# A hybrid DeltaNet and attention layer on one core: gates and rotation from PSUM, a mask by TensorE, wider spacing of dependent products, and a last stage one tile ahead

## The chip, the core and the metric

The kernel runs on one core of a Trainium2 chip. TensorE multiplies into PSUM, VectorE and ScalarE read PSUM, GpSimd works on SBUF only, and SyncE's queue starts most DMA transfers. The metric is device time per execution, in microseconds (us): 1606.91, the median of three runs (1602.01, 1608.14, 1606.91). Lower is better.

## The reference, cut to what matters

```python
mod = silu(c) @ w_mod + b_mod                    # shift, scale, gate
h = rmsnorm(x, norm_w) * (1 + scale) + shift     # (2048, 1024)
proj = h @ w_in      # DeltaNet q,k,v and gate z, its beta and decay, attention q,k,v and gate z
dn_qkv = silu(causal_short_conv(dn_qkv, conv_w)) # 4 heads x 128; q and k are l2-normalised
o_dn = gated_delta_rule(q, k, v, g, beta)        # per chunk: decay exp(g_c - g_s) for s <= c,
                                                 # inverse of a unit triangular matrix, state S
o_dn = rmsnorm(o_dn, dn_norm_w) * silu(dn_z)
aq, ak = rope(at_q, positions), rope(at_k, positions)
o_at = dilated_attention(aq, ak, av)             # 8 heads x 64, windows with strides 1, 4, 16, joined by log-sum-exp
o_at = rmsnorm(o_at, at_norm_w) * silu(at_z)
x = x + gate * (concat(o_dn, o_at) @ w_out)
return rmsnorm(x, final_norm_w)
```

Everything is float32. The kernel takes a large product as three: each operand is split into a part `hi` that float32r holds exactly and a rest `lo`, and hi*hi, hi*lo and lo*hi are added up in PSUM.

## The kernel before

The 2048 tokens are taken in two halves of two blocks of 512. There are four stages.

- **Start** (to about 160 us): modulation, normalised x, first projections.
- **Projections with DeltaNet** (to about 1095 us): the main stream, `rest` and `dn_unit`, makes one projection after another, each 24 products of 128x128 by 128x512 into a bank `ip` (two buffers). Sixteen DeltaNet units (4 heads x 4 blocks) run beside it.
- **Hand-over** (to about 1135 us): `mix_first` multiplies `NM` token tiles of the DeltaNet output by w_out, 24 products a tile, and adds x; attention's operands are loaded.
- **Attention** (to about 1495 us) and the **last stage**: `attention` runs 128 pieces of scores, softmax, transposes and values. `mix_dn` (the DeltaNet tiles that `mix_first` left) and then `mix_at` (the attention half of the output, final RMSNorm, 16 tiles) are generators in the queue `side`, stepped beside it as `FILL` says, and alone once attention is out of pieces.

A DeltaNet unit is a chain of small dependent products: `dn_intra` (decay matrix, gram products), `dn_solve` (16x16 inverses on VectorE), `dn_double` (inverse doubled to 32, 64 and 128 in TensorE products named `g<-...`), and `dn_scan` (four chunks, each `sc<-state,kq`, then `sc<-y,inv`, then `sc<-y,kdec` and `sc<-y,qk`; VectorE or ScalarE makes the next operand in between), then `dn_out`. Each part sits in a queue of its own; `tick` steps the first generator of each queue once per step of the main stream. Between dependent products a generator waits in `hop(n)` until the main stream has issued n x 1.1 us of estimated TensorE work (`spent`), or, where the main stream has nothing to issue, 0.3 us of such credit per tick. A unit may not start its projections before the unit four places earlier is through (`done[0] < n - KQ + 1`), and waits in `dn_intra` until its set of buffers is free (`u["need"]`). A scheduler then orders the instructions by its own model of when each can start, so the final order differs from the order of the code. Each engine works through its own in order.

Names that the change touches: `DB0`, `DB1`, `DB2`, `SC1`, `SC2`, `SC3` are the n of the hops of `dn_double` and `dn_scan`; `z_gate` makes silu(z) from a projection's bank; `rope_unit` rotates q and k; `gate_row` computes the modulation's gate.

Of the kernel before, what the change touches and what calls it, by code (L numbers as in the profile page):

```python
# [11 lines left out]
F32 = mybir.dt.float32  # L12
# [9 lines left out]
P = 128  # L22
# [17 lines left out]
DB0 = 2.5  # L40
DB1 = 2.0
DB2 = 2.0
SC1 = 2.5
SC2 = 1.5
SC3 = 1.5
# [11 lines left out]
NM = 4  # L57
# [32 lines left out]
FILL = (1, 0)  # L90
# [22 lines left out]
def kernel(ctx: ExitStack, tc: tile.TileContext, x, c_t, pos, w_mod, b_mod_t, b_gate,  # L113
# [110 lines left out]
    gt_r = persist.tile([P, P], F32R, name="gt_r")  # L224
    cw = persist.tile([P, 12, 4], F32, name="cw")
# [457 lines left out]
    def z_gate(pool, ps, col, dst):  # L683

        zr = pool.tile([P, J], F32, name="z_r", tag="t512", bufs=T5)
# [116 lines left out]

    def dn_double(pool, u, xct):
# [17 lines left out]
        yield from hop(DB1)  # L821
# [10 lines left out]
        yield from hop(DB0)  # L832
        for lvl in range(2):
# [14 lines left out]
            yield from hop(DB1)  # L848
# [8 lines left out]
            yield from hop(DB2)  # L857
        grown[0] += 1

    def dn_scan(fa, pool, h, j, u, gt_, gz):  # L860
# [6 lines left out]
        for c in range(4):  # L867
# [6 lines left out]
            yield from hop(SC1)  # L874
# [3 lines left out]
            yield from hop(SC2)  # L878
# [7 lines left out]
            yield from hop(SC3)  # L886
        tail.append(dn_out(fa, pool, h, j, o, so, u["eq"], gz))

    def dn_out(fa, pool, h, j, o, so, eq, gz):
# [13 lines left out]
        V.tensor_tensor(oc, ps.rearrange("p c t -> p (c t)").rearrange("p (i r) -> p r i", r=4),  # L903
                        g.rearrange("p (r i) -> p r i", r=4), OP.mult)
# [28 lines left out]
    def dn_unit(fa, h, js, hs, gt_, launch, ahead=None):  # L933
        wk, wv = [load_unit(2 * h + i) for i in range(2)] if not ahead else (None, ahead[0])
        for jj in range(2):
# [16 lines left out]
            z_gate(fa, (yield from proj(wv, hs[jj], 1)), 0, gz)  # L952
# [30 lines left out]
    def z_part(pool, u, j, ct, ps):  # L983
        gz = pool.tile([P, J], F32, name="z_at", tag="t512", bufs=T5)
        z_gate(pool, ps, 1, gz)
# [12 lines left out]
    def rope_unit(fa, u, js, hs, w):  # L998
        w = w or load_unit(u)
        scr = (qscr, kscr)[u >= 10][u % 2]  # L1000
        for jj in range(2):
# [6 lines left out]
            xs = []  # L1008
            for ct in range(2):
                ps = yield from proj(w, hs[jj], ct)  # L1010
                t = fa.tile([P, J], F32, name="rx", tag="t512", bufs=T5)
                A.copy(t.rearrange("p (r i) -> p r i", r=4), ps.rearrange("p (i r) -> p r i", r=4))  # L1012
                xs.append(t)
                yield
            for ct in range(2):
                p1 = fa.tile([P, J], F32, name="rp1", tag="t512", bufs=T5)
                p2 = fa.tile([P, J], F32, name="rp2", tag="t512", bufs=T5)
                V.tensor_tensor(p1, xs[ct], tab[0], OP.mult)
# [222 lines left out]
    def combine(pool, p, blk, oa, ob, sta, sb):  # L1241
# [47 lines left out]
        V.tensor_tensor(oc, ps, flat(gz), OP.mult)  # L1289
# [150 lines left out]
    for half in range(2):  # L1440
# [6 lines left out]
        for h in range(HD):  # L1447
            run(dn_unit(fa, h, js, hs, gts[half], launch, None if half or h else (wv, kqs)))
            if half == 0 and h == 1:
# [64 lines left out]
    with tc.tile_pool(name="mix", bufs=2, side="right", reuse_waits="tile") as mp:  # L1514
        with tc.tile_pool(name="att", bufs=2, side="left", reuse_waits="tile") as ap_:
# [32 lines left out]
            def mix_at():  # L1548
# [8 lines left out]
                yield from hop(MIXLAG2)  # L1557
                for i in range(16):
                    t = 4 * (i % 4) + i // 4
                    while combined[i // 4] < 4:  # L1560
                        yield
                    y = ya[:, i % 4]
                    dma(y, yscr[t // 4, (t % 4) * P:(t % 4 + 1) * P, :])
                    ss = ap_.tile([P, 4], F32, name="f_ss", bufs=4)

                    def use(n, ps):
# [3 lines left out]
                        A.activation(sq, y[:, c], AF.Square, accum_out=ss[:, n:n + 1])  # L1570
                        if n == 0:
                            V.tensor_scalar(ss[:, 0:1], ss[:, 0:1], 1.0 / D, EPS, op0=OP.mult, op1=OP.add)

                    oc = yb[:, 1 + i // 2 % 3, i % 2 * J:i % 2 * J + J].rearrange("p (k i) -> p k i", k=4)
                    yield from mix(*halves("m_x", MX), load_o(oc, t, 4), wa, use, lambda: bank("s", SB) if over else bank("ip", IP2))
                    V.scalar_tensor_tensor(ss[:, 2:3], ss[:, 1:2], 1.0 / D, ss[:, 0:1], op0=OP.mult, op1=OP.add)
                    G.tensor_tensor(y[:, J:D], y[:, J:D], fw[:, J:D], OP.mult)
                    rsqrt(ap_, ss[:, 3:4], ss[:, 2:3], "f")
                    V.scalar_tensor_tensor(y[:, 0:J], y[:, 0:J], ss[:, 3:4], fw[:, 0:J], op0=OP.mult, op1=OP.mult)  # L1579
                    A.activation(y[:, J:D], y[:, J:D], AF.Copy, scale=ss[:, 3:4])  # L1580
                    for c in ((slice(0, J), slice(J, D)) if i == 15 else (slice(0, D),)):
                        nc.scalar.dma_start(class_rows(t, out)[:, c], y[:, c])
# [104 lines left out]
```

## Time and profile before

| | |
|---|---|
| profiled execution, its own time | 1607.58 us (span of its instructions 1605.7) |
| median of three runs | 1606.91 us |
| TensorE products (PE) | 1448.7 us busy, 90% of the span |
| VectorE (DVE) | 1125.1 us, 70% |
| ScalarE (ACT) | 674.5 us, 42% |
| GpSimd (POOL) | 497.7 us, 31% |
| mean granted TensorE clock | 0.963 of full |

Busy PE counts each product from start to end, and neighbours overlap; the time from one product to the next is shorter than its duration. A wait of PE in the rows is idle time, put down to what ended it. [...]

### The profile page before, as it was taken

To read this page: it belongs to the slowest core of one execution; us is meant where nothing else is said; L and a number is where in the kernel's file an instruction comes from. 1 tells how busy PE (TensorE), PEld (TensorE's weight loads), DVE (VectorE), ACT (ScalarE), POOL (GpSimd) and SP (SyncE) were. 2 spreads that over 40 slices of the span, in tenths; PEclk is the share of its full clock that TensorE was granted. 3 is DMA by queue.
4 is the path that set the end of the run, shared out by engine and by line. 5 is a ranking of instruction groups with operands and counts; after the bars stand their busy time and mean duration, and the time that the engine had idled before them with its cause. 6 is when DMAs were issued, how large, how long until landed. Compare 5 with 4: busy or idle time off the path is not lost. (4 is left out here: it accounts for less than half of the span.)

```text
span 1605.7 us, 28520 instructions
## 1 busy us (share of the span) xinstructions
PE 1448.7 (90%) x9832; PEld 1166.6 (73%) x9832; DVE 1125.1 (70%) x3478; ACT 674.5 (42%) x1894; POOL 497.7 (31%) x589
## 2 busy tenths in 40 slices
PE   3898899799879878999999999997899999999986
PEld 3686778667667767877877688876677777777764
DVE  6858825796775776676777767435476686898887
ACT  3534224324233664424324243222455555666443
POOL 2324352354462424133142321213121221142333
PEclk9989999999999988999999999998999999999998
DMA  8745551755552652161442424437877637264353
GB/s 253 255 134 177 163 170 56 246 165 179 166 183 89 222 160 90 53 191 57 147 139 79 149 74 148 148 114 237 252 214 214 198 109 235 82 197 113 120 191 129
DMA packets 255184, 252.89 MB, mean 157 GB/s; under 512 B 44864, under 2 KB 196544, under 8 KB 254528
## 3 DMA queue, kind: packets, MB, share of 16 engines
q1 hardware_dynamic: 252592, 242.69, 48.8%
q10 hardware_dynamic: 2448, 8.39, 1.3%
q8 instruction: 78, 1.28, 0.3%
q14 instruction: 66, 0.54, 0.1%
HBM read 160.12 MB, written 90.90 MB: 156 GB/s over the span
## 5 line engine op out<-in xcount | busy, mean ns | idle before, releaser
L149 PE MATMUL ip<-h_hi,w_hi 128*128 128x512 f32 x864 | 355.9, 413 | 1.5 <-ACT z_r L689 1.5
L149 PE MATMUL ip<-h_hi,w_lo 128*128 128x512 f32 x864 | 355.8, 413 | 0.0
L149 PE MATMUL ip<-h_lo,w_hi 128*128 128x512 f32 x864 | 354.5, 412 | 0.0
L149 PEld LDWEIGHTS ip<-h_hi,w_hi 128*128 128x128 f32 x864 | 167.1, 194 | 33.8 <-ACT z_r L689 2.2
L149 PEld LDWEIGHTS ip<-h_hi,w_lo 128*128 128x128 f32 x864 | 166.6, 193 | 32.3 <-issue 0.5
L149 PEld LDWEIGHTS ip<-h_lo,w_hi 128*128 128x128 f32 x864 | 166.9, 193 | 31.9 <-issue 0.2
L675 DVE SCALAR_TENSOR_TENSOR cv_y<-cv_r,cw,cv_y 128x512 f32<-128x512 f32 x144 | 117.1, 813 | 41.0 <-ACT cv_y L672 37.1
L561 POOL TENSOR_TENSOR w_lo<-w_raw,w_hi 128x512 fp32r<-128x512 f32 x72 | 98.1, 1372 | 128.3 <-ACT w_hi L560 106.3
L1204 DVE CUSTOM_DVE_ANT_0 sm<-s,mask 128x256 f32<-128x256 f32 (+3 forms) x256 | 107.8, 446 | 19.3 <-PE s L149 14.0
L154 PE MATMUL tr<-cst,p 128*128 128x128 f32 x568 | 94.3, 287 | 3.4 <-ACT p L1207 1.7
L1229 DVE COPY pts<-tr 128x512 f32<-128x512 f32 (+1 forms) x120 | 72.9, 615 | 33.7 <-PE tr L154 32.6
L1207 ACT ACTIVATE p<-sm,sta 128x256 f32<-128x256 f32 (+1 forms) x128 | 63.2, 495 | 71.2 <-DVE sta L1204 60.4
L1207 ACT ACTIVATE p<-sm,stb 128x128 f32<-128x128 f32 (+3 forms) x128 | 70.9, 555 | 50.2 <-DVE stb L1204 37.3
L154 PEld LDWEIGHTS tr<-cst,p 128*128 128x128 f32 x568 | 61.7, 142 | 25.0 <-issue 15.8
L149 PE MATMUL ip<-w_hi,h_hi 128*128 128x264 f32 (+1 forms) x256 | 76.8, 300 | 2.8 <-ACT v_at L138 1.5
L149 PE MATMUL ip<-w_hi,h_lo 128*128 128x264 f32 (+1 forms) x256 | 76.9, 300 | 0.0
L149 PE MATMUL ip<-w_lo,h_hi 128*128 128x264 f32 (+1 forms) x256 | 76.8, 300 | 0.0
L789 DVE TENSOR_TENSOR tmp_inv<-xt_inv,blk 128x8 f32<-128x8 f32 (+14 forms) x240 | 67.2, 280 | 5.8
L677 ACT ACTIVATE cv_t<-cv_y 128x512 f32<-128x512 f32 x48 | 30.3, 632 | 82.9 <-DVE cv_y L675 62.3
L560 ACT CAST w_hi<-w_raw 128x512 fp32r<-128x512 f32 x72 | 43.5, 619 | 50.6 <-DMA w_raw<-in_w_in_dram 25.8
L1019 POOL TENSOR_TENSOR rp<-rx,tab 128x512 f32<-128x512 f32 x32 | 43.3, 1366 | 58.0 <-ACT rx L1012 51.2
L138 ACT ACTIVATE sqo<-o 128x128 f32<-128x128 f32 x64 | 19.8, 309 | 93.4 <-DVE o L138 84.0
(464 smaller groups left out, 3497.3 us busy)
## 6 DMA issues: line engine op xcount, KB each, us to landing
w_raw<-in_w_in_dram SPq DMA_DIRECT2D x72, 256.0 KB, 4.0
ws<-w_hi SPq DMA_DIRECT2D x15, 1024.0 KB, 5.5
ws<-w_lo SPq DMA_DIRECT2D x15, 1024.0 KB, 7.1
w_hi<-ws SPq DMA_DIRECT2D x15, 1024.0 KB, 5.8
w_lo<-ws SPq DMA_DIRECT2D x15, 1024.0 KB, 7.4
xt<-in_x_dram SPq DMA_DIRECT2D x16, 512.0 KB, 4.7
wm<-in_w_mod_dram SPq DMA_DIRECT2D x32, 256.0 KB, 5.5
tab<-ctab SPq DMA_DIRECT2D x32, 256.0 KB, 3.5
```

The lines of the kernel that those rows point to most:

```text
L138: return f(*a, **k)
L149: i = self.engine.matmul(ps, lhsT=lhsT, rhs=rhs, **k)
L154: i = self.engine.transpose(*a)
L560: A.copy(hi[:, s, 0:256], raw)
L561: G.tensor_tensor(lo[:, s, 0:256], raw, hi[:, s, 0:256], OP.subtract)
L675: V.scalar_tensor_tensor(y, r[:, n:n + J], cw[:, ti, n:n + 1], y, op0=OP.mult, op1=OP.add)
L677: A.activation(t, y, AF.Tanh)
L789: V.tensor_tensor(tmp[:, :, 0:i + 1], xt[:, :, 0:i + 1], b3[:, i:i + 1, 0:i + 1].to_broadcast([P, 4, i + 1]), OP.mult)
L1019: G.tensor_tensor(p2, xs[1 - ct], tab[1], OP.mult)
L1204: V.tensor_tensor_reduce(out=sm, in0=pp[hd], in1=masks, scale=-0.125, scalar=BIG, op0=OP.add, op1=OP.min, accum_out=st[:, slot, hd:hd + 1])
L1207: A.activation(pt, sm, AF.Exp, scale=-1.0, bias=st[:, slot, hd:hd + 1], accum_out=st[:, slot, 2 + hd:3 + hd])
L1229: V.tensor_copy(pts[:, 0:kn], pt[:, 0:kn])
```

## The change

1. `z_gate`: ScalarE's copy of the bank (scaled by a norm weight) goes; VectorE's product reads the bank itself. The norm weight is applied in `dn_out` and `combine`, where a two-operand product becomes a three-operand one.
2. `rope_unit`: the product with the cosines is made from the bank right after the projection; ScalarE's copy stays for the other product.
3. `dn_intra`: GpSimd's multiplication of the decay matrix by a triangular mask goes; a third product into the same bank, of -1e30 times the identity with the strict triangle, sends the masked exponents to minus infinity before the exponential.
4. The hops of `dn_double` and `dn_scan` grow for the units 0 to 13: doubling from 2.0 (one 2.5) to 4.0, scan from 2.5, 1.5 and 1.5 to 4.0, 3.0 and 3.5. The last two units keep the short ones.
5. `mix_first` takes eight tiles and not four (`NM`), and beside attention every third step works on `side`, not every second (`FILL`).
6. `mix_at` loads and splits tile i+1 before the products of tile i, and makes the final norm's reciprocal roots for two tiles at once.
7. `gate_row` moves from the second head of the first half to the first head of the second half.

```diff
-DB0 = 2.5
-DB1 = 2.0
-DB2 = 2.0
-SC1 = 2.5
-SC2 = 1.5
-SC3 = 1.5
+DB = (4.0, 2.0)
+SC1 = (4.0, 2.5)
+SC2 = (3.0, 1.5)
+SC3 = (3.5, 1.5)
+SHORT = 14
-NM = 4
+NM = 8
-FILL = (1, 0)
+FILL = (1, 0, 0)
...
+        V.tensor_scalar(off_r, ident, -1.0e30, None, op0=OP.mult)
...
     def z_gate
         A.activation(t.rearrange("p (r i) -> p r i", r=4), by_class, AF.Tanh, scale=0.5)
-        A.activation(zr.rearrange("p (r i) -> p r i", r=4), by_class, AF.Copy, scale=nwz[:, col:col + 1])
-        V.scalar_tensor_tensor(dst, t, 1.0, zr, op0=OP.add, op1=OP.mult)
+        V.scalar_tensor_tensor(dst.rearrange("p (r i) -> p r i", r=4), t.rearrange("p (r i) -> p r i", r=4), 1.0,
+                               by_class, op0=OP.add, op1=OP.mult)
...
     def dn_intra
         for i in range(2):
-            T.matmul(psd, lhsT=gt_r, rhs=gm[i], start=i == 0, stop=i == 1)
+            T.matmul(psd, lhsT=gt_r, rhs=gm[i], start=i == 0, stop=False)
+        T.matmul(psd.rearrange("p (c t) -> p c t", c=4), lhsT=off_r, rhs=gt_r[:, None, :].to_broadcast(B),
+                 start=False, stop=True)
         A.activation(flat(em), psd, AF.Exp)
-        G.tensor_tensor(em, em, le[:, None, :].to_broadcast(B), OP.mult)
...
+    def short(u):
+        return u["n"] >= SHORT
...
-            yield from hop(SC1)
+            yield from hop(SC1[short(u)])
...
     def rope_unit
+                p1 = fa.tile([P, J], F32, name="rp1", tag="t512", bufs=T5)
+                V.tensor_tensor(p1.rearrange("p (r i) -> p r i", r=4), by_class,
+                                tab[0].rearrange("p (r i) -> p r i", r=4), OP.mult)
...
-                V.tensor_tensor(p1, xs[ct], tab[0], OP.mult)
...
     def mix_at
+                nxt = parts(0)
                 for i in range(16):
...
+                    y, o = nxt if nxt else parts(i)
+                    nxt = None
+                    yield
+                    if i + 1 < 16 and combined[(i + 1) // 4] == 4:
+                        nxt = parts(i + 1)
...
-                    rsqrt(ap_, ss[:, 3:4], ss[:, 2:3], "f")
+                    if e or i >= 14:
+                        m = slice(0, 2) if i < 14 else slice(e, e + 1)
...
+                        rsqrt(ap_, rs[:, m], ss[:, 2, m], "f")
+                        for j, yj in pair if i < 14 else pair[-1:]:
+                            close(j, yj, rs[:, j % 2:j % 2 + 1])
```

Three places show what the final order makes of it. The first is TensorE in the fourth chunk of the scan of unit 1 (`sc<-y,inv`, then `sc<-y,kdec` and `sc<-y,qk`; the `ip` rows are projections). Before:

```order
L149 MATMUL sc<-y_2964,inv 128x128
L149 MATMUL ip<-h_lo,w_hi 128x512
L149 MATMUL ip<-h_hi,w_lo 128x512
L149 MATMUL ip<-h_hi,w_hi 128x512
L149 MATMUL ip<-h_lo,w_hi 128x512
L149 MATMUL ip<-h_hi,w_lo 128x512
L149 MATMUL ip<-h_hi,w_hi 128x512
L149 MATMUL ip<-h_lo,w_hi 128x512
L149 MATMUL ip<-h_hi,w_lo 128x512
L149 MATMUL sc<-y,kdec 128x128
L149 MATMUL sc<-y,qk 128x128
```

The same chunk in the changed kernel, from the product ahead of it:

```order
L149 MATMUL sc<-state_72,kq 128x128 x2
L149 MATMUL ip<-h_hi,w_lo 128x512
L149 MATMUL ip<-h_hi,w_hi 128x512
L149 MATMUL ip<-h_lo,w_hi 128x512
L149 MATMUL ip<-h_hi,w_lo 128x512
L149 MATMUL sc<-y_3261,inv 128x128
L149 MATMUL ip<-h_hi,w_hi 128x512
L149 MATMUL ip<-h_lo,w_hi 128x512
L149 MATMUL sc<-y,kdec 128x128
L149 MATMUL sc<-y,qk 128x128
```

Here eight projections stood between the two dependent steps, and two stand there now. In the second chunk of the same unit it went the other way, from eight to sixteen.

The second place is SyncE's queue as attention is opened. The names: `oscr` and `yscr` are outputs in memory, `k_lo` and `k_hi` attention's keys, `mask` its mask, `q` and `va` its queries and values. Before:

```order
L905 DMA oscr_120<-oc 512x1x128
L1136 DMA yscr<-mf_x 128x512
L1488 DMA mask<-in_const_dram 128x768
L1136 DMA yscr<-mf_x 128x512
L1132 DMA mf_x<-in_x_dram 128x512
L1147 DMA k_lo<-kscr_79 128x1x512
```

In the changed kernel:

```order
L1145 DMA yscr<-mf_x 128x512 x4
L910 DMA oscr_121<-oc 512x1x128
L1497 DMA mask<-in_const_dram 128x768
L1156 DMA q<-qscr_82 128x1x512
L1191 DMA va<-vscr 32x4x128 x4
L1193 DMA vb<-vscr 128x4x128
```

The mask's load stood ahead of the last tiles' stores and of most key loads; now it is behind all of them and behind the last DeltaNet output, and the keys are loaded earlier.

The third place is ScalarE in the last stage (`m_hi` is the split of a tile, `f_sq` the squares of the one being finished, `out_dram` its store). Before:

```order
L1570 ACTIVATE f_sq,f_ss<-y_hi 128x512
L1101 CAST m_hi<-y_lo 128x512
L1570 ACTIVATE f_sq,f_ss<-y_hi 128x512
L1580 ACTIVATE y_hi<-y_hi,f_ss 128x512
L1582 DMA out_dram<-y_hi 128x1024
```

In the changed kernel:

```order
L1610 ACTIVATE f_sq,f_ss<-y_hi 128x512
L1579 CAST m_hi<-y_lo 128x512
L1610 ACTIVATE f_sq,f_ss<-y_hi 128x512
L1579 CAST m_hi<-y_lo 128x512
L1610 ACTIVATE f_sq,f_ss<-y_hi 128x512 x2
L1586 ACTIVATE y_hi<-y_hi,f_rs 128x512 x2
L1588 DMA out_dram<-y_hi 128x1024 x2
```

The split of a tile stood behind both squares of the tile before; now it stands one tile earlier, and two tiles are closed together.

## Rows read from the trace of the kernel before

**Rows 1.** Busy time by stretch, the granted clock behind the five engines.

```profile
core 0: us, PE busy (x) PEld busy (x) DVE busy (x) ACT busy (x) POOL busy (x), PEclk, DMA share, GB/s
660.00:1060.00 400.00, 390.30 (x2793) 316.12 (x2791) 270.50 (x861) 137.00 (x414) 108.89 (x169) 0.99 0.38 122
1135.00:1495.00 360.00, 343.09 (x2750) 271.54 (x2752) 274.50 (x1044) 204.70 (x641) 84.43 (x84) 0.98 0.59 173
```

**Rows 2.** PE's waits between 160 and 1060 us: total, times, longest.

```profile
PE g L149 <- DVE w L138: 14.9, 7, 6.4
...
PE sc L149 <- DVE state L138: 7.1, 8, 1.6
...
PE sc L149 <- ACT y L138: 3.6, 4, 2.0
PE g L149 <- DVE tmp_inv L789: 3.5, 1, 3.5
PE sc L149 <- ACT o L138: 3.0, 4, 1.0
PE g L149 <- DVE xc L138: 2.2, 3, 1.0
```

**Rows 3.** Single waits of PE in time: start, duration, idle before in brackets.

```profile
216.84 0.96 PE L149 MATMUL g<-xd,w 32*32 32x32 f32 x16 [2.60 <-DVE w L138]
...
434.88 0.49 PE L149 MATMUL sc<-y,kdec 128*128 128x128 f32 x2 [2.01 <-ACT y L138]
...
474.72 0.96 PE L149 MATMUL g<-xd,w 32*32 32x32 f32 x16 [6.36 <-DVE w L138]
...
558.29 0.49 PE L149 MATMUL sc<-y,kdec 128*128 128x128 f32 x2 [0.53 <-ACT y L138]
...
603.83 0.64 PE L149 MATMUL g<-x,kk 32*32 32x32 f32 x16 [3.54 <-DVE tmp_inv L789]
608.01 1.08 PE L149 MATMUL g<-xc,kk 64*64 64x64 f32 x8 [0.84 <-DVE xc L138]
609.71 0.65 PE L149 MATMUL g<-inv,w 64*64 64x64 f32 x4 [0.61 <-DVE w L138]
...
808.50 0.49 PE L149 MATMUL sc<-y,kdec 128*128 128x128 f32 x2 [0.64 <-ACT y L138]
```

**Rows 4.** Busy time and granted clock in two stretches behind long waits.

```profile
217.00:224.00 7.00, 6.92 (x49) 6.49 (x48) 0.39 (x2) 2.21 (x7) 5.76 (x5) 0.51 0.57 187
603.00:613.00 10.00, 7.72 (x72) 6.97 (x73) 8.53 (x39) 6.35 (x17) 4.44 (x9) 0.50 0.04 15
```

**Rows 5.** A piece of the chain that ended last, in attention: start, us, what.

```profile
1203.56 0.93 PE ip L149 x4
```

**Rows 6.** Single waits of PE at the hand-over.

```profile
1113.04 0.50 PE L149 MATMUL ip<-w_hi,mf_lo 128*128 128x512 f32 x1 [0.77 <-POOL mf_lo L1102]
...
1135.29 0.47 PE L149 MATMUL s<-k_hi,q_lo 128*128 128x128 f32 x1 [3.06 <-DVE sta L1321]
```

**Rows 7.** The mask's load, by tile: time from issue to landing.

```profile
DMA to landing us min/median/max: 6.4/6.4/6.4
```

**Rows 8.** Products of the last stage, by tile: durations, first and last start.

```profile
L149 PE MATMUL s<-w_hi,m_lo x120: 387/389/501, 1495.7 to 1593.4; 128*128 128x512 f32 x120
```

**Rows 9.** PE's waits between 1495 and 1606 us.

```profile
PE s L149 <- POOL m_lo L1102: 10.0, 10, 1.3
```

**Rows 10.** The last stage's chain: one step of the reciprocal root.

```profile
1547.37 1.20 DVE rs_u L280
```

**Rows 11.** VectorE's groups by line: busy, mean ns, idle before.

```profile
L1018 DVE TENSOR_TENSOR rp<-rx,tab 128x512 f32<-128x512 f32 x32 | 27.1, 848 | 0.0
...
L690 DVE SCALAR_TENSOR_TENSOR z_at<-z_t,z_r 128x512 f32<-128x512 f32 x16 | 12.0, 755 | 7.4 <-ACT z_r L689 6.8 <-issue 0.6
...
L903 DVE TENSOR_TENSOR oc<-tr,g 128x512 f32<-128x512 f32 x16 | 10.9, 684 | 10.1 <-PE tr L154 9.8
```

**Rows 12.** The same for GpSimd's split in the last stage.

```profile
L1102 POOL TENSOR_TENSOR m_lo<-y_lo,m_hi 128x512 fp32r<-128x512 f32 x16 | 20.4, 1273 | 17.8 <-ACT m_hi L1101 17.7
```

More of the change, by code (lines that the diff above doesn't have):

```diff
@@ L224 @@
     gt_r = persist.tile([P, P], F32R, name="gt_r")
+    off_r = persist.tile([P, P], F32R, name="off_r")
     cw = persist.tile([P, 12, 4], F32, name="cw")
@@ L820, in dn_double @@
         AE.copy(w, ps)
-        yield from hop(DB1)
+        yield from hop(DB[short(u)])
         ps = blocks(x, w)
@@ L831, in dn_double @@
             GE.tensor_copy(xc[q, :, q], x[q])
-        yield from hop(DB0)
+        yield from hop(DB[short(u)])
         for lvl in range(2):
@@ L856, in dn_double @@
                 AE.copy(xct[f, :, s], pt[f])
-            yield from hop(DB2)
+            yield from hop(DB[short(u)])
         grown[0] += 1
@@ L877, in dn_scan @@
             AE.copy(y, a[:, 2])
[L878 removed]
+            yield from hop(SC2[short(u)])
             b = bank("sc").rearrange("p (c t) -> p c t", c=4)
@@ L1448 @@
             run(dn_unit(fa, h, js, hs, gts[half], launch, None if half or h else (wv, kqs)))
-            if half == 0 and h == 1:
+            if half == 1 and h == 0:
                 aux.append(gate_row(fa))
@@ L1557, in mix_at, with tile_of, parts, close @@
                 yield from hop(MIXLAG2)
-                for i in range(16):
[L1559 to L1564, printed above, removed]
+                def tile_of(i):
+                    return 4 * (i % 4) + i // 4
+                def parts(i):
+                    oc = yb[:, 1 + i // 2 % 3, i % 2 * J:i % 2 * J + J].rearrange("p (k i) -> p k i", k=4)
+                    load_o(oc, tile_of(i), 4)
+                    y = ya[:, i % 4]
+                    t = tile_of(i)
+                    dma(y, yscr[t // 4, (t % 4) * P:(t % 4 + 1) * P, :])
+                    hi, lo = halves("m_x", MX)
+                    A.copy(hi, oc)
+                    G.tensor_tensor(lo, oc, hi, OP.subtract)
+                    return y, (hi, lo)
+                def close(i, y, rs):
+                    t = tile_of(i)
+                    V.scalar_tensor_tensor(y[:, 0:J], y[:, 0:J], rs, fw[:, 0:J], op0=OP.mult, op1=OP.mult)
+                    A.activation(y[:, J:D], y[:, J:D], AF.Copy, scale=rs)
+                    for c in ((slice(0, J), slice(J, D)) if i == 15 else (slice(0, D),)):
+                        nc.scalar.dma_start(class_rows(t, out)[:, c], y[:, c])
+                while combined[0] < 4:
+                    yield
+                nxt = parts(0)
+                for i in range(16):
+                    y, o = nxt if nxt else parts(i)
+                    nxt = None
+                    yield
+                    if i + 1 < 16 and combined[(i + 1) // 4] == 4:
+                        nxt = parts(i + 1)
+                    if i % 2 == 0:
+                        ss = ap_.tile([P, 3, 2], F32, name="f_ss", bufs=2)
+                        rs = ap_.tile([P, 2], F32, name="f_rs", bufs=2)
+                        pair = []
+                    e = i % 2
+                    pair.append((i, y))
                     def use(n, ps):
@@ L1569, in use @@
                         sq = ap_.tile([P, J], F32, name="f_sq", tag="sm", bufs=SMB)
[L1570 to L1576, printed above, removed]
-                    G.tensor_tensor(y[:, J:D], y[:, J:D], fw[:, J:D], OP.mult)
-                    rsqrt(ap_, ss[:, 3:4], ss[:, 2:3], "f")
[L1579 to L1582, printed above, removed]
+                        A.activation(sq, y[:, c], AF.Square, accum_out=ss[:, n, e:e + 1])
+                    for n in range(2):
+                        b = bank("s", SB) if over else bank("ip", IP2)
+                        yield from three(b, [lambda k, p=p: o[p][:, k] for p in range(2)],
+                                         [lambda k, p=p: wa[k // 2][p][:, k % 2, n * J:n * J + J] for p in range(2)], 4)
+                        use(n, b)
+                        yield
+                    G.tensor_tensor(y[:, J:D], y[:, J:D], fw[:, J:D], OP.mult)
+                    if e or i >= 14:
+                        m = slice(0, 2) if i < 14 else slice(e, e + 1)
+                        V.tensor_tensor(ss[:, 2, m], ss[:, 0, m], ss[:, 1, m], OP.add)
+                        V.tensor_scalar(ss[:, 2, m], ss[:, 2, m], 1.0 / D, EPS, op0=OP.mult, op1=OP.add)
+                        rsqrt(ap_, rs[:, m], ss[:, 2, m], "f")
+                        for j, yj in pair if i < 14 else pair[-1:]:
+                            close(j, yj, rs[:, j % 2:j % 2 + 1])
+                    while i < 15 and combined[(i + 1) // 4] < 4:
+                        yield
             ahead["v"] = load_v(ap_, 0, 0)
```

25 lines of the change are left out of this document (13 added, 12 removed).

## The prediction

> **What bounds the kernel now.** I read four views in this order: busy time by stretch, the waits of TensorE by what ended them, single waits in time, and the last stage by tile. By stretch, TensorE is busy 390.3 of 400 us in the second half of the projections and 343.1 of 360 us in attention [rows 1]; VectorE is behind it there with 270.5 and 274.5 us. So the reader is to take TensorE as the bound through most of the program: a product added or removed counts at its pitch, and everything else counts only where TensorE waits for it. The pitch is 0.93 us for four products of width 512, 0.232 us each [rows 5]. The waits show three places where TensorE isn't fed. In the projections the six largest that stand behind a DeltaNet operand come to 14.9 + 7.1 + 3.6 + 3.5 + 3.0 + 2.2 = 34.3 us [rows 2]; the single ones shown run from 0.53 to 6.36 us [rows 3]. At the hand-over a tile waits 0.77 us for its rest part, and attention's first product 3.06 us [rows 6]. In the last stage ten tiles wait 10.0 us for the same rest part [rows 9]. [...]
>
> I count against the profiled execution, 1607.6 us, which is 0.7 us above the median of the three runs. A measurement of this kernel tells about 0.5% from no change, 8 us; that is the bound below.
>
> **The mask on TensorE.** Sixteen units get one more product of width 512: 16 x 0.232 = **+3.7 us**, all of it on the bound engine. GpSimd's product goes; nothing waited for it in the rows, so it gives nothing by itself.
>
> **Gates and rotation from PSUM.** ScalarE loses 32 copies; TensorE's waits for them are few and the bank is now free when VectorE is through, not ScalarE. A bank is held longer by VectorE's product of 0.684 us (a product that reads PSUM, [rows 11]) and by its queue, while the other bank's projection lasts 24 x 0.232 = 5.6 us, so this is hidden; if VectorE lags more than that, its queue shows up as TensorE waiting for a product of the gate. I take 0, with -2 to +3 us. The rows say that VectorE itself gains: reading the bank took 0.684 us where the products with two operands in SBUF took 0.848 (rotation) and 0.755 us (gate) [rows 11], so 32 x 0.164 + 16 x 0.071 = 6.4 us less VectorE time. [...]
>
> **The hops.** I counted the order of both kernels. There are 191 steps between dependent products of the scan and 80 of the doubling. With fewer than eight projections between them (1.86 us) there were 22 of 271 before; there are **75 of 271** now. The reason is the rule for a unit's start. The chain of a unit grows by 4 x 5.0 hops in the scan and 11.5 in the doubling, 31.5 x 1.1 = 35 us of estimated TensorE work, so units end later, the main stream reaches `done[0] < n - KQ + 1` before they are through, and then nothing is left to put between the products but what the scheduler pulls forward. The other 196 steps are wider, mostly sixteen to twenty-four projections in place of eight to sixteen. Price of a tight step: in the rows five of the 22 waited, 0.53 + 3.54 + 0.84 + 0.61 + 0.64 = 6.2 us [rows 3], 0.28 us a step. Its bounds are 0 (a step that always arrives in time) and 6.2 / 5 = 1.23 us (every tight step waits as those did). I take 0.28, since the scheduler places a tight step where it expects the operand. The wide steps carry the rest, 34.3 - 6.2 = 28.1 us. With 1.8 us more between them only what exceeds 1.8 us stays: 4.56 of 6.36, 0.80 of 2.60 and 0.21 of 2.01, 5.6 us, times 196/249 = 4.4 us. So 75 x 0.28 + 4.4 = 25.4 against 34.3: **-8.9 us**. The low clock behind the 2.60 us goes (-3.5), one more like that behind the 3.54 us is likely among three times as many tight steps (+3.9): 0.
>
> **The hand-over.** Four tiles, 96 products or 22.3 us, move from attention to the hand-over. TensorE is the bound on both sides, so the move itself is 0. What is late next: in attention a tile's rest part is ready while the scores run; in `mix_first` each tile waits for it, 4 x 0.77 = 3.1 us [rows 6]. The DeltaNet chain, whose end had 108 wide products behind it, now has only 20 and the last unit's output, so the mask's load is issued behind the last store. It took 6.4 us [rows 7]; the first scores hide about 3 of it, and before the change 3.06 us were lost at this place: about +2 more. Queued behind the mask on SyncE are the queries and values, for which attention waits next. Together **+5 us**, with 0 (the longer hand-over hides the key loads) to +15 (below).
>
> **The last stage.** Before, 15 tiles run from 1495.7 to 1593.6 us, 6.53 us a tile [rows 8], where 24 products need 5.57. The split of tile i+1 now stands a tile earlier on ScalarE, so the rest part (1.27 us on GpSimd, [rows 12]) is made beside products. The order has 15.5 tiles in this stage: 15.5 x 5.57 = 86.3 us against 97.9, and half a tile less in attention, 2.8 us: **-14.4 us**. What comes behind the last product, 12 us to the end of the span at 1605.7, keeps its length. Next in line is VectorE: a pair of tiles has four sums and two products of about 0.7 us, ten small steps of a root, and one of them that took 1.20 us beside GpSimd [rows 10] where such a step alone is near 0.2, some 8 us in 11.1. [...]
>
> **The sum.** 3.7 - 8.9 + 5 - 14.4 = -14.6: 1607.6 - 14.6 = **1593 us**. `gate_row` moves 16 VectorE products from one half to the other; TensorE waits for neither: 0.
>
> **Rivals.**
> - *Starvation (slower).* The change asks for more projections between the products and gets fewer: in the tight stretches TensorE waits at every step. For it: 75 tight steps against 22, and the half-speed clock behind long waits. Against it: 17 of the 22 tight steps before didn't wait. At 0.75 us a step the DeltaNet part is 56.3 + 4.4 - 34.3 = +26.4 and the kernel, with the other three terms at 3.7 + 5 - 14.4 = -5.7, 1607.6 - 5.7 + 26.4 = 1628 us. It decides from 0.58 us a step: 43.5 + 4.4 - 34.3 - 5.7 = +8.
> - *Just in time (faster).* The scheduler's model fits: tight steps cost nothing, only 4.4 us of waits stay (-29.9), and both low-clock stretches go (-7.4): 1607.6 - 5.7 - 37.3 = 1565 us, or half of that, 1583 us.
> - *The entry into attention.* TensorE stands for the mask's whole load, 6.4 us, and then runs 10 us at half clock (3.9 us): 10.3 more than forecast, 1603 us, no change.
>
> **Chances.** Forecast 0.46, with its own range of 1580 to 1606 (faster 0.30, within 0.5% 0.15, slower 0.01). Just in time 0.25, all faster. Starvation 0.18 (slower 0.16, same 0.02). Entry 0.11 (same 0.07, slower 0.04). So faster 0.55, same 0.24, slower 0.21. The range is 1570 to 1628 us: the lowest part of the second case and the upper half of the third are left out.
>
> **What would show it.** The last stage: tiles 5.5 to 5.7 us apart and TensorE's waits for the rest part below 2 us; if they stay at 6.5, that step is wrong. The masks: 16 products with `off_r`, the same pitch. The hops: waits for DeltaNet operands between 160 us and the hand-over of 20 to 40 us in total; above 55 starvation is right, below 12 the second rival. The hand-over: a first wait of attention between 4 and 8 us. The prediction fails most easily by the price of a tight step, which rests on five waits.

## The result and the profile after

The changed kernel takes **1580.43 us** (median of four runs, 1578.94 to 1581.32) against 1605.79 for the kernel before on the same chip: a ratio of 0.9843, 95% interval 0.9821 to 0.9866. Run a second time, on another occasion, it took 1580.06 us (five runs), ratio 0.9825 (0.980 to 0.985). It is faster by 25 to 28 us where 14.6 were forecast; the range held the time. The profiled execution took 1579.6 us with a span of 1577.8.

The stages of the changed kernel, cut where the stretches of before were cut. The windows show, behind the five engines' busy time, the granted clock as a share of full speed (PEclk):

```profile
core 0: us, PE busy (x) PEld busy (x) DVE busy (x) ACT busy (x) POOL busy (x), PEclk, DMA share, GB/s
...
160.00:660.00 500.00, 461.95 (x3036) 373.44 (x3036) 315.89 (x980) 198.88 (x542) 173.63 (x228) 0.98 0.47 152
660.00:1070.00 410.00, 391.02 (x2859) 314.38 (x2858) 274.02 (x884) 127.30 (x396) 97.80 (x165) 0.97 0.40 127
1070.00:1146.00 76.00, 65.57 (x315) 51.62 (x313) 34.89 (x84) 17.96 (x49) 19.34 (x16) 0.98 0.75 241
1146.00:1482.00 336.00, 319.58 (x2652) 252.84 (x2652) 264.18 (x1020) 201.01 (x633) 77.28 (x78) 0.98 0.57 166
```

The same two stretches of the projections, and the hand-over, before:

```profile
160.00:660.00 500.00, 447.59 (x3044) 362.60 (x3043) 341.63 (x1019) 203.09 (x561) 195.63 (x239) 0.95 0.48 152
660.00:1070.00 410.00, 399.85 (x2841) 324.14 (x2840) 275.80 (x879) 140.63 (x425) 112.45 (x171) 0.99 0.39 124
...
1095.00:1135.00 40.00, 28.18 (x104) 20.77 (x102) 16.72 (x30) 7.06 (x14) 11.44 (x9) 0.87 0.72 217
```

In the first 500 us of the projections the granted clock rose from 0.95 to 0.98, an estimated 15 us of full-speed work, and in the next 410 it fell from 0.99 to 0.97, 8 us given back; the profile of the second occasion has 0.97 and 0.98, so a hundredth is also what the same kernel varies by. The last projection starts 17.3 us earlier than before (1078.15 for 1095.43). Attention's first product stands at 1145.8 us, 10.5 later than before, although four tiles (22.3 us) were moved ahead of it. Attention is 25 us shorter, which is what the four and a half tiles that left it need. TensorE's waits from 158 to 1078 us (total, times, longest) answer to [rows 2]:

```profile
PE g L149 <- DVE w L138: 7.0, 4, 4.9
PE sc L149 <- ACT o L138: 6.8, 3, 3.4
...
PE g L149 <- DVE xc L138: 4.0, 1, 4.0
PE g L149 <- DVE gb L344: 3.2, 1, 3.2
PE g L149 <- POOL gmghi L700: 2.8, 1, 2.8
PE g L149 <- DVE g L645: 2.5, 1, 2.5
PE g L149 <- DVE xd L138: 2.2, 1, 2.2
...
PE sc L149 <- DVE state L138: 1.8, 4, 0.7
...
PE sc L149 <- ACT y L138: 1.4, 2, 0.8
```

The rows of `w`, `o`, `xc`, `xd`, `state` and `y` come to 23.2 us, 25 with three that are under 1.2 us; 34.3 before. The other three, 8.5 us, are new: the kernel before has no such wait. `g` and `gmghi` are inputs of the decay matrix; `gb` is a sum of `gate_row`, which holds the bank that the next DeltaNet product needs. All of TensorE's waits before the last projection, of whatever kind, come to 62 us before, to 56 here and to 55 in the second profile. At the hand-over the single waits answer to [rows 6]. Six tiles wait for the rest part; the first product of attention waits 0.84 us and the next group 3.49, behind a VectorE instruction that had itself waited for the mask's load (last line, from the waits of all engines; the load took 4.3 us):

```profile
1091.16 0.51 PE L149 MATMUL ip<-w_hi,mf_lo 128*128 128x512 f32 x1 [0.78 <-POOL mf_lo L1111]
...
1145.81 0.33 PE L149 MATMUL s<-k_hi,q_lo 128*128 128x128 f32 x1 [0.84 <-DVE sta L1330]
...
1151.44 0.33 PE L149 MATMUL s<-k_hi,q_hi 128*128 128x128 f32 x1 [3.49 <-DVE sta L1213]
```
```profile
DVE sm L1213 <- DMA mask<-in_const_dram: 5.0, 1, 5.0
```

The products of the last stage by tile (durations, first and last start) answer to [rows 8], their one wait to [rows 9]:

```profile
L149 PE MATMUL s<-w_hi,m_lo x124: 388/389/497, 1481.7 to 1567.7; 128*128 128x512 f32 x124
```
```profile
PE s L149 <- POOL m_lo L1580: 0.6, 1, 0.6
```

86.0 us for 15.5 tiles, 5.55 a tile, and 10 us behind the last product where there were 12.

### The profile page after: what moved, and what is told of

It reads as the page before. It is cut to its first block, busy times and chain, and to the rows that moved or that the text cites. A ratio compares the mean times of both kernels' runs of the same rounds, so it can differ in the third digit from the quotient of the medians.

```text
span 1577.8 us, 28423 instructions
## 1 busy us (share of the span) xinstructions
PE 1443.6 (91%) x9848; PEld 1162.6 (74%) x9848; DVE 1073.0 (68%) x3395; ACT 656.9 (42%) x1862; POOL 460.1 (29%) x573
## 5 line engine op out<-in xcount | busy, mean ns | idle before, releaser
L149 PE MATMUL ip<-h_hi,w_hi 128*128 128x512 f32 x864 | 350.9, 408 | 2.0 <-DVE gz L690 1.6
L677 DVE SCALAR_TENSOR_TENSOR cv_y<-cv_r,cw,cv_y 128x512 f32<-128x512 f32 x144 | 112.6, 782 | 35.1 <-ACT cv_y L674 31.3
L154 PE MATMUL tr<-cst,p 128*128 128x128 f32 x568 | 98.1, 288 | 4.8 <-ACT p L1216 3.9
L791 DVE TENSOR_TENSOR tmp_inv<-xt_inv,blk 128x8 f32<-128x8 f32 (+14 forms) x240 | 58.8, 245 | 6.2
```

What stands on the lines that cost most here:

```text
L149: i = self.engine.matmul(ps, lhsT=lhsT, rhs=rhs, **k)
L154: i = self.engine.transpose(*a)
L677: V.scalar_tensor_tensor(y, r[:, n:n + J], cw[:, ti, n:n + 1], y, op0=OP.mult, op1=OP.add)
L791: V.tensor_tensor(tmp[:, :, 0:i + 1], xt[:, :, 0:i + 1], b3[:, i:i + 1, 0:i + 1].to_broadcast([P, 4, i + 1]), OP.mult)
```

## The experiments

Each part was taken out of the changed kernel or put alone into the one before. The changed kernel run beside three of them says how well its own time is known.

**after_again**: no edit.

> The changed kernel once more, unedited, on the same chip as the three beside it, so that differences of a few us can be told. Every theory: 1578 to 1583; how far its runs spread says how large a difference of the hops' edit can be read at all.

Measured: 1580.06 us, 1577.80 to 1582.26. With the first four, nine runs lie between 1577.8 and 1582.3; medians that differ by less than about 3 us are not told apart.

### The last stage

**old_last**: `mix_at` as before, `NM` and `FILL` as changed.

```diff
-                nxt = parts(0)
                 for i in range(16):
-                    y, o = nxt if nxt else parts(i)
...
-                    if i + 1 < 16 and combined[(i + 1) // 4] == 4:
-                        nxt = parts(i + 1)
...
+                    oc = yb[:, 1 + i // 2 % 3, i % 2 * J:i % 2 * J + J].rearrange("p (k i) -> p k i", k=4)
+                    yield from mix(*halves("m_x", MX), load_o(oc, t, 4), wa, use, lambda: bank("s", SB) if over else bank("ip", IP2))
```

> The changed kernel with the last stage's loop of before (each tile's load, halves and products in one piece; NM and FILL as changed). Recorded price of the loop: 15.5 tiles by 6.31 - 5.57 us, and half a tile more left for the stage's end, which comes to +14.4 us, so 1594 to 1595, with waits for m_lo back at about 10 us. Theory B: half of the shorter stage is due to the two further tiles moved into the hand-over and to the attention's shares (FILL), not to the loop, and the time is 1585 to 1589.

Measured: 1597.41 us, ratio to before 0.9954 (0.9934 to 0.9973), **+17** against the changed kernel. The projections and attention are the same to 4 us; the last stage's products now take 101.6 us, and TensorE waits for the rest part in 13 tiles:

```profile
L149 PE MATMUL s<-w_hi,m_lo x124: 388/389/501, 1484.9 to 1586.5; 128*128 128x512 f32 x124
```
```profile
PE s L149 <- POOL m_lo L1111: 12.4, 13, 1.3
```

Theory A: the loop itself carries the gain.

### The distances between dependent products

**short_hops**: `SHORT = 14` becomes `SHORT = 0`.

> The changed kernel with SHORT at 0, so that every DeltaNet unit uses the distances of before (2.0 to 2.5 projections in the doubling, 2.5, 1.5 and 1.5 in the scan); all else is the changed kernel. Theory A (the recorded price): the distances gain only the 8.9 us of waits, so the time is 1580.4 + 9 = about 1589, and the stretches at granted clock 0.5 before the hand-over stay near the 44 us of the changed kernel. Theory B (the second rival's price): waits and half-clock stretches come and go together, so the stretches go back to about 61 us, half of the difference being time, and the time is 1595 to 1600. Theory C: the distances gain nothing, and what was gained before the attention comes from the lighter engines; the time is 1578 to 1583.

Measured: 1582.08 us (1577.82 to 1588.93), 0.9854 (0.982 to 0.9888): +2, not told apart from nothing; theory C. The profiled execution was a long one, 1587.4 us, and in it the waits of the kinds counted above are back at 36 us (`w` alone 14.8). But the waits for `gb`, `gmghi` and `g` are gone with the wide distances, and all waits before the last projection come to 60 us against 56 and 55; engines_only (below), which has the short distances too, has 55. So the wide distances exchange one kind of wait for another, and no trace shows that they take any away.

**tight_hops**: `DB`, `SC1`, `SC2`, `SC3` all `(1.0, 1.0)`.

> The changed kernel with every distance of the doubling and the scan at 1.0 projection, a stronger dose of what short_hops did: in the program's order the median of projections between two dependent products falls from 12 to 8, and 17 of them have 16 to 31 (124 in the changed kernel). Theory A (distance has a price): the waits for DeltaNet operands, 25 us in the changed kernel and 36 us with the distances of before, come to 45 to 60 us, and the time is 1595 to 1615. Theory B (an operand that is late comes from a full queue on VectorE or ScalarE and not from the distance): the waits stay at 25 to 38 us and the time at 1579 to 1588.

Measured: 1581.98 us (1579.32 to 1589.07), 0.9841 (0.9816 to 0.9867). Even this dose costs nothing that shows: theory B. Other waits took the place of those for `w`: `o` 11.0, `xc` 5.5, `xt_inv` 5.2 us, read in the longest of its six executions; all waits before the last projection come to 58 us.

**hops_only**: the kernel before with the new distances alone.

```diff
-DB0 = 2.5
-DB1 = 2.0
...
+DB = (4.0, 2.0)
+SC1 = (4.0, 2.5)
+SC2 = (3.0, 1.5)
+SC3 = (3.5, 1.5)
+SHORT = 14
```

> The kernel before with the changed kernel's distances alone (DB, SC1 to SC3, SHORT at 14). Theory A (the recorded price): the DeltaNet waits fall by about 9 us, so 1605 - 9 = 1596. Theory B: the distances are worth 0 to 3 us by themselves, as taking them out of the changed kernel cost 1.6: 1602 to 1606. Theory C: with ScalarE's copies and GpSimd's mask still there, the operands come late at the wider distances too, and the tight steps of the last units cost more than is saved: 1607 to 1612.

Measured: **1622.88 us**, 1.0095 (1.0068 to 1.0122): 15 us slower than before, against every theory on record, since even C expected less. Projections end 3 us earlier (1092.0 for 1095.4) and attention begins 6 us later (1141.7 for 1135.3). Counting TensorE's products behind the last projection gives the reason for that: none of the scan's before, 64 here. The hand-over is 9.8 us longer by it (49.7 for 39.9). Another 8 us of the profiles' difference stand behind attention's first product; their cause stays open. The next two pairs of runs take the hand-over up.

### The hand-over

**nm4**: `NM = 4`, `FILL = (1, 0)` in the changed kernel.

> The changed kernel with NM at 4 and FILL at (1, 0), so four tiles (22.3 us of products) go from the hand-over back to the attention and the last stage. Theory A (the recorded price): the hand-over loses 4 waits of 0.77 us and about 2 us at the entry, while half a tile more (2.8 us) lands in the attention's shares or the last stage without costing in sum: 1580.4 - 5 = about 1575. Theory B: the further tiles fill TensorE where it otherwise waits at the hand-over and keep its clock at 1.0 (7 us at half clock there in the changed kernel, 14 before), so without them the time is 1583 to 1588.

Measured: 1594.83 us, 0.9919 (0.9895 to 0.9944): **+15**, the other side of the recorded +5, and more than theory B. In the profiles attention begins 19 us earlier than in the changed kernel (1126.8 for 1145.8 us), though 22.3 us of products are gone ahead of it, and from there to the end it takes 31 us longer (462.7 for 432.0). So of the 11.7 us by which the profiled execution is longer, 4.7 are lost in the hand-over, which shrinks by 17.6 us and not by 22.3, and 8.4 behind it; its projections end 1.4 us earlier. Behind it the granted clock is lower, here in nm4 and then in the changed kernel:

```profile
1200.00:1300.00 100.00, 95.77 (x752) 74.69 (x750) 72.62 (x278) 52.77 (x165) 20.46 (x21) 0.98 0.60 182
1300.00:1400.00 100.00, 95.69 (x758) 75.07 (x757) 73.96 (x279) 54.19 (x170) 16.75 (x18) 0.97 0.51 150
```
```profile
1200.00:1300.00 100.00, 97.12 (x810) 77.23 (x807) 80.45 (x315) 58.27 (x184) 21.39 (x23) 1.00 0.65 186
1300.00:1400.00 100.00, 96.48 (x812) 75.43 (x812) 79.53 (x299) 58.76 (x183) 17.34 (x19) 1.00 0.50 145
```

That is an estimated 5 us of the 8.4. Whether `FILL` or the tiles do it was not separated.

**no_last** and **engines_only**: the changed kernel with `mix_at` as in old_last and `NM` and `FILL` as in nm4, all three as before. The second has the short distances as well, so that masks, gates, rotation and `gate_row` alone are left of the change:

```diff
-SHORT = 14
+SHORT = 0
```

> The changed kernel without its last part: the loop of before in the last stage, NM at 4 and FILL at (1, 0); masks, gates, rotation, gate_row and distances as changed. Either half of that part alone cost about 15 us when undone (17.3 for the loop, 14.8 for NM). Theory A (the halves are separate terms): 1580 + 17 + 15 = 1612. Theory B (the tile ahead and the tiles moved to the hand-over cover the same loss, so that either needs the other): 1594 to 1599. Theory C (distances and NM belong together: a DeltaNet chain that is stretched runs on after the last projection, where only the hand-over's further tiles stand beside it, as hops_only's 15 us say): 1605 to 1615, with attention's first product 10 us and more behind the last projection's usual 40 us.

> The kernel no_last with SHORT at 0, that is the kernel before with masks on TensorE, gates and rotation from PSUM and the later gate_row alone (the doubling's first distance is 2.0 where it was 2.5). Theory A (undoing them one by one in the changed kernel cost 6.4 and 3.0 us): 1605 - 9 = 1596. Theory B (they are worth something only beside the wider distances): 1602 to 1606. Against no_last it is the price of the distances where the hand-over has 4 tiles: theory C of no_last says no_last is slower by 10 to 15 us, theories A and B say it is equal or faster by 2 to 9.

Measured: no_last 1608.45 us, 1.0006 (0.999 to 1.0021); engines_only 1597.48 us, 0.9951 (0.9934 to 0.9969). engines_only came out as its theory A. Where the hand-over has four tiles the distances cost 9 us (by the ratios, 0.0055 x 1606): theory C of no_last. Its trace shows how. The scan's last product of each chunk and the hand-over's third product, with durations and first and last start:

```profile
L149 PE MATMUL sc<-y,qk x16: 275/275/421, 1072.5 to 1125.1; 128*128 128x128 f32 x16
```
```profile
L149 PE MATMUL ip<-w_hi,mf_lo x32: 388/393/628, 1085.9 to 1115.7; 128*128 128x512 f32 x32
```

The last projection is at 1081.4 us. The four tiles are over at 1115.7, the scan runs on to 1125.1 with nothing beside it, and attention's first product comes at 1132.0, behind the transposes of the scan's output. TensorE's waits there, and its busy time and clock:

```profile
1119.59 0.49 PE L149 MATMUL sc<-y,inv 128*128 128x128 f32 x2 [0.84 <-ACT o L138]
1120.43 0.49 PE L149 MATMUL sc<-y,kdec 128*128 128x128 f32 x2 [0.36 <-ACT y L138]
...
1129.93 1.11 PE L154 MATMUL tr<-cst,o 128*128 128x128 f32 x4 [4.42 <-POOL o L902]
```
```profile
1120.00:1130.00 10.00, 3.59 (x16) 2.54 (x16) 3.22 (x16) 1.71 (x7) 1.04 (x1) 0.62 0.19 58
```

In engines_only the scan's last product is at 1081.6 us, ahead of the last projection. In the changed kernel the scan ends even later than in no_last, but eight tiles last longer than it:

```profile
L149 PE MATMUL sc<-y,qk x14: 275/275/275, 1078.6 to 1139.1; 128*128 128x128 f32 x14
...
L149 PE MATMUL ip<-w_hi,mf_lo x64: 387/394/628, 1082.6 to 1143.6; 128*128 128x512 f32 x64
```
```profile
1126.00:1136.00 10.00, 9.13 (x46) 7.40 (x45) 3.00 (x7) 1.68 (x6) 1.28 (x1) 1.00 0.81 263
```

TensorE is busy for 9.13 us of ten at full clock there, where in no_last it was 3.59 at 0.62.

The time from the last projection to attention's first product says what tiles and distances do to the hand-over, in the profiles (last_all is the next run):

| tiles at the hand-over | distances | us |
|---|---|---|
| 4 | short | 39.9 (before), 36.2 (engines_only) |
| 4 | wide | 49.7 (hops_only), 50.5 (no_last), 50.1 (nm4) |
| 8 | short | 64.5 (last_all), 64.5 (short_hops) |
| 8 | wide | 67.7 (changed kernel), 67.1 (after_again) |

Four further tiles, 22.3 us of products, add 25 to 28 us with the short distances and 17 to 18 with the wide ones. The wide distances add 10 to 14 us beside four tiles and 3 beside eight.

**last_all**: the kernel before with the new `mix_at`, `NM = 8` and `FILL = (1, 0, 0)`, and nothing else.

> The kernel before with the last part alone: the loop that works one tile ahead, NM at 8, FILL at (1, 0, 0). Theory A (the recorded terms): hand-over +5 and last stage -14.4, so 1605 - 9.4 = 1596. Theory B (the further tiles stand beside work that leaves TensorE waiting, and so gain as much as the loop does): -14 to -20, 1585 to 1591.

Measured: 1588.01 us, 0.9889 (0.9872 to 0.9906): -18, theory B. The combinations that were run, as ratios to before (the new second and third column without the first is missing):

| masks, gates, rotation, `gate_row` | last stage, `NM`, `FILL` | distances | ratio (95%) |
|---|---|---|---|
| new | before | before | 0.9951 (0.9934 to 0.9969) |
| before | new | before | 0.9889 (0.9872 to 0.9906) |
| before | before | new | 1.0095 (1.0068 to 1.0122) |
| new | before | new | 1.0006 (0.999 to 1.0021) |
| new | new | before | 0.9854 (0.982 to 0.9888) |
| new | new | new | 0.9843 (0.9821 to 0.9866) |

The first column is worth 8 us alone, 6 beside the second and 14 beside the third, the second 16 to 18 with the short distances and 26 with the wide ones, the third +15 alone, +9 beside the first, and nothing that shows beside both.

### Masks, gates and rotation

**scalar_copies**: the copies and the product from SBUF are back.

```diff
+        zr = pool.tile([P, J], F32, name="z_r", tag="t512", bufs=T5)
+        A.activation(zr.rearrange("p (r i) -> p r i", r=4), by_class, AF.Copy, scale=1.0)
+        V.scalar_tensor_tensor(dst, t, 1.0, zr, op0=OP.add, op1=OP.mult)
...
+                V.tensor_tensor(p1, xs[ct], tab[0], OP.mult)
```

> The changed kernel with the gate's second factor and the rotation's first product read from ScalarE's copies in SBUF again (the gate's copy has scale 1, the weight stays in the later product). Theory A (the recorded price): 0, so 1578 to 1583. Theory B: PSUM is released later and ScalarE carries 32 or more copies again, which delays the projections' banks; this is where the 10 us before the attention that the sum doesn't have come from: 1585 to 1591. [...]

Measured: 1586.79 us (1584.03 to 1592.25), 0.9887 (0.9861 to 0.9914): **+6**, theory B, in time. In VectorE's groups the rotation's product takes 978 ns from SBUF in the mean and took 687 from PSUM, the gate's 719 and 680 (the medians are closer: the rotation's are in the last section, the gate's are 692 ns in the kernel before and 678 in the changed one):

```profile
L1025 DVE TENSOR_TENSOR rp<-rx,tab 128x512 f32<-128x512 f32 x32 | 31.3, 978 | 7.3 <-ACT rx L1019 5.3 <-DMA tab<-ctab 2.0
...
L692 DVE SCALAR_TENSOR_TENSOR gz<-z_t,z_r 128x512 f32<-128x512 f32 x16 | 11.5, 719 | 8.0 <-ACT z_r L691 8.0
```

The changed kernel:

```profile
L1020 DVE TENSOR_TENSOR rp<-ip,tab 128x512 f32<-128x512 f32 x32 | 22.0, 687 | 32.7 <-ACT rx L1018 31.4 <-DMA tab<-ctab 1.3
L908 DVE SCALAR_TENSOR_TENSOR oc<-tr,nwz,g 128x512 f32<-128x512 f32 x16 | 12.0, 748 | 3.2 <-issue 2.5 <-PE tr L154 0.5
...
L690 DVE SCALAR_TENSOR_TENSOR gz<-z_t,ip 128x512 f32<-128x512 f32 x16 | 10.9, 680 | 5.7 <-ACT z_t L689 5.7
```

With the copies TensorE also waits for them at the bank: 5.4 us for `z_r` and 4.5 for `v_at` over the whole run, where the changed kernel has 4.2 for `z_at` and `gz` and 0.9 for `v_at`.

**gpsimd_mask**: the third product goes, GpSimd's mask is back.

```diff
-            T.matmul(psd, lhsT=gt_r, rhs=gm[i], start=i == 0, stop=False)
...
+            T.matmul(psd, lhsT=gt_r, rhs=gm[i], start=i == 0, stop=i == 1)
...
+        G.tensor_tensor(em, em, le[:, None, :].to_broadcast(B), OP.mult)
```

> The changed kernel with the mask of em as a GpSimd product behind the exponential again, and without the third TensorE product. Theory A (the recorded price): 16 products of 0.232 us go from TensorE, which is full there, and nothing waits for GpSimd: 1580.4 - 3.7 = about 1577. Theory B: GpSimd's product is on the way to the DeltaNet operands or holds VectorE up, and the waits for them grow by more than the 3.7 us: 1582 to 1590.

Measured: 1583.47 us (1582.46 to 1585.08), 0.9862 (0.9836 to 0.9887): **+3**, theory B, by less than 4 us. Its five runs lie above all nine of the changed kernel, but the intervals of the ratios overlap: that the mask on TensorE costs the forecast 3.7 us is out (0.982 would be expected here), and that it gains 3 is at the edge of what can be told. The clock says nothing: it is 0.97 from 160 to 660 us, and the changed kernel has 0.98 and 0.97 there in its two profiles. TensorE's waits before the last projection come to 61 us against 56 and 55; the largest kind, 8.5 us, is for VectorE's roots. VectorE is busy for longer with the same number of instructions, first here, then in the changed kernel (1075.2 in its second profile):

```profile
PE 1442.7 (91%) x9832; PEld 1165.1 (74%) x9832; DVE 1081.6 (68%) x3395; ACT 657.0 (42%) x1862; POOL 484.6 (31%) x589
```
```profile
PE 1443.6 (91%) x9848; PEld 1162.6 (74%) x9848; DVE 1073.0 (68%) x3395; ACT 656.9 (42%) x1862; POOL 460.1 (29%) x573
```

### A version that follows from it

**lo_last**: in the hand-over a tile waits for its rest part after two products. Here the eight products that don't need it go first.

```diff
-            yield from three(b, [lambda k, p=p: o[p][:, k] for p in range(2)],
-                             [lambda k, p=p: w[k // 2][p][:, k % 2, n * J:n * J + J] for p in range(2)], 4)
+            i = 0
+            for q, p, k in [(0, p, k) for k in range(4) for p in range(2)] + [(1, 0, k) for k in range(4)]:
+                T.matmul(b, lhsT=o[q][:, k], rhs=w[k // 2][p][:, k % 2, n * J:n * J + J], start=i == 0, stop=i == 11)
```

> The changed kernel with one edit of its own, in mix (hand-over and DeltaNet tiles of the attention): the eight products of a half tile that read only the upper part of the activations go first, and the four that read the lower part, which GpSimd makes, after them. The wait for mf_lo comes 8 products (1.86 us) into a tile instead of 2 (0.46 us). Theory A (that wait, 0.77 us in 7 of 8 tiles, sets the hand-over's pace): its 4.9 us go and the time is 1575 to 1577. Theory B (the tile then waits for the next thing, the load or the sum into mf_x): the wait for mf_lo goes, another comes, and the time is 1579 to 1582.

Measured: **1576.34 us** (1574.19 to 1578.48), 0.9808 (0.9789 to 0.9826), the fastest run here; against the changed kernel about -4, though the two intervals overlap. Half of B came true as well: no product waits for `mf_lo`, but one now waits for the sum into `mf_x`:

```profile
1105.56 0.77 PE L149 MATMUL ip<-w_hi,mf_hi 128*128 128x512 f32 x1 [3.81 <-DVE mf_x L1148]
```

From the last projection to attention it is 65.5 us, 67.7 in the changed kernel.

## Why the prediction was right in direction and short in size

- **By place**, in the two profiles: the last projection starts 17.3 us earlier, where 3.7 - 8.9 = -5.2 was forecast; the hand-over is 27.8 us longer, where 22.3 + 5 was forecast; attention is 24.5 us shorter, where 22.3 + 2.8 was; the last stage with what follows it is 13.9 us shorter, where 11.6 was. So the 13 us that the forecast lacks stand almost all in the projections. The hand-over agrees by luck, as its term below shows.
- **The bound** held: TensorE, and what it isn't fed with. The forecast priced that in waits. The clock belongs to the same price, and was taken as 0: 7 us net between 160 and 1070 us, by the clocks shown above (15 gained, 8 given back), 6 in the second profile. The -3.5 and +3.9 us behind that 0 are the author's estimate, half of TensorE's busy time at the clocks of 0.51 and 0.50 in [rows 4]; no run shows either by itself.
- **The last stage** held: 5.57 us a tile forecast, 5.55 measured; -14.4 forecast, 17 lost when undone.
- **The masks** were mis-sized, +3.7 forecast and 0 to -3 measured. The sixteen products are there, 406 ns each; "nothing waited for it in the rows, so it gives nothing by itself" is the sentence that is in doubt. No engine's idle time is put down to GpSimd's product (1.31 us behind each exponential) in either trace that has it, so that part of the reading was right; what the run with it has more of is VectorE time, 6 to 9 us, and waits of TensorE for VectorE. What makes VectorE's time longer there was not isolated.
- **Gates and rotation** were mis-sized, 0 forecast with -2 to +3, about -6 measured. The rows had the shorter products (6.4 us less VectorE time), and the step let them count for nothing since TensorE is the bound; but TensorE's waits at the banks, 9.9 us with the copies, are 5.1 without them. The traces have the rotation's product at a median of 692 ns from PSUM (changed kernel) and of 684 and 686 from SBUF (before, scalar_copies), 6 to 8 ns apart the other way. The prediction's "VectorE itself gains" holds for the means alone.
- **The hops**: the kinds of waits that the forecast counted came out as forecast, 25 us for 25.4, and tight steps didn't starve TensorE. But those kinds were a choice: the transposes that wait for `sqj` and `vs`, DeltaNet's as well, were larger before (6.2 and 4.6 us) than four of "the six largest", and in the changed kernel three new kinds add 8.5 us. All waits fell by 6 to 7 us, and by as much in engines_only with the short distances. The term of -8.9 is not there. In the changed kernel it is 0 to -5, and by itself the edit costs 9 to 15. What the step left out: a longer chain ends later. It moved 64 scan products from beside the projections to behind the last one. In the profiles with four tiles the last projection starts 2 to 3 us earlier by it and the hand-over is 10 to 14 us longer.
- **The hand-over**: +5 forecast for four more tiles, -15 measured by nm4. The waits for the rest part were right (4.5 us in six tiles). The sign that was named, a first wait of attention of 4 to 8 us, was not seen: it was 0.84, and 4.3 with the next one. "TensorE is the bound on both sides, so the move itself is 0" was wrong: with the wide distances the hand-over holds a chain that leaves TensorE idle, and four tiles put there cost 17 to 18 us for 22.3 us of products. The prediction had seen the chain's end move ("now has only 20" wide products behind it) and priced only the mask's load by it. This is 4.7 of the 11.7 us by which nm4's profile is longer; 8.4 stand behind attention's first product, go with a lower clock there and are not explained. Against the kernel before, two terms cancel: the distances lengthen a hand-over of four tiles by 10 to 14 us, for which the sum has nothing, and the tiles give back about 5 of that.
- **`gate_row`** was put at 0 because TensorE waits for none of its products. It does now, once, 3.2 us for `gb`; in engines_only, which has the later `gate_row` beside short distances, it doesn't.
- By stages of one sum, with the ratios times 1606: masks, gates and rotation -8 for +3.7; hand-over and last stage on top of them -16 for -9.4; the distances on top of both 0 to -5 for -8.9. Two terms too low and one too high: that the range held the time is in part such a balance.

The rivals: starvation is out, with waits for DeltaNet operands of 25 us, 34 with the new kinds, and not above 55, and tight_hops, with every distance below those of both kernels, lost nothing that shows. Just in time has the right time (1565 to 1583) but not its cause: 25 us of waits stayed, not 4.4. The entry into attention came true in part: VectorE idles 5.0 us until the mask has landed, TensorE for 3.5 us, and the granted clock is 0.85 in the ten us from 1146, where the rival had 6.4 us and half clock.

Open: why the first group keeps the clock up. It ends the projections 12 us earlier (1083.3 for 1095.4 in engines_only), takes 62 us of TensorE's waits between 160 us and the last projection to 55 and the clock from 0.97 to 0.98, but which of its edits breaks which wait was not separated, and `gate_row` was not undone by itself. Nor were `NM` and `FILL` undone apart.

## What to carry to other kernels

Before a chain is spread out, look where it ends: work put between its steps is free only while there is work, and the chain's last units pay behind it. Two edits that look like separate terms may be one, as wide distances and further tiles at the hand-over are here: price them together or run the four combinations. When a change is to take waits away, compare the sum of all waits in the stretch and not the kinds that were there before: here the old kinds fell as forecast, and new ones came. And on an engine that is full on the average, a product need not cost its pitch: TensorE's sixteen products for the mask, 3.7 us by their pitch, cost nothing that shows here (1580.43 us with them, 1583.47 without).

## What was not expected of the hardware

- By the median the rotation's product on VectorE was about as long from SBUF, 684 and 686 ns, as from PSUM, 692; only from SBUF were some far longer, up to 1825 and 2862 ns. The product (durations: least, median, most) in the kernel before, in scalar_copies and in the changed kernel:

```profile
L1018 DVE TENSOR_TENSOR rp<-rx,tab x32: 650/684/1825, 185.4 to 1058.6; 128x512 f32<-128x512 f32 x32
```
```profile
L1025 DVE TENSOR_TENSOR rp<-rx,tab x32: 651/686/2862, 182.9 to 1040.8; 128x512 f32<-128x512 f32 x32
```
```profile
L1020 DVE TENSOR_TENSOR rp<-ip,tab x32: 652/692/694, 169.7 to 1036.3; 128x512 f32<-128x512 f32 x32
```

  The means, 848 ns [rows 11] and 978 from SBUF against 687 from PSUM, come from a few long ones: in the kernel before 6 of the 32 lasted over 0.75 us, 0.77 to 1.82, and every one of them ran beside a GpSimd instruction. Those from PSUM had GpSimd beside them for about 12 of their 22.0 us, and none was over 694 ns.
- The product of `oc`, 128x512, went from 684 ns with two operands [rows 11] to 748 with the weight as a third; the sixteen in the changed kernel take 744 to 754.
- Kernels that make the same projections run them at other clocks: from 160 to 660 us the mean was 0.95 before, 0.96 in engines_only, 0.97 in scalar_copies, and 0.98 and 0.97 in two profiles of the changed kernel. One hundredth is 5 us there, more than most of the waits by operand shown above, and no more than one kernel varies by.
